# A third seven-product quad for the short convolution's x and C, earlier loads for the retention heads, and an earlier join in w_o

## The chip, the cores and the metric

The kernel runs on one core of one Trainium2 chip. The metric is the device time of one execution in microseconds. The median of three runs of the kernel before is 1023.01 us (1022.69 to 1025.45).

## The reference

One encoder block for x of 512 tokens by 1024 features, float32. Cut to what the change touches:

```python
h = rmsnorm(x, g_mix)
proj = h @ w_in
xc, gb, gc, q, k, v, g_sw, gate_a, gate_r = split(proj)
u = gc * xc
conv = sum over 3 taps of shifted u * w_conv[tap]
y_a = (gb * conv) @ w_a_out
ret = retention(rotary(q), rotary(k), v), 4 heads, normalised per head
y_r = (ret * g_ret * silu(g_sw)) @ w_r_out
x = x + (sigmoid(gate_a) * y_a + sigmoid(gate_r) * y_r) @ w_o
h2 = rmsnorm(x, g_ffn)
x = x + (silu(h2 @ w_ff_gate) * (h2 @ w_ff_up)) @ w_ff_down
y = rmsnorm(x, g_final)
```

xc, gb and gc are 1024 columns wide each; in the kernel they are x, B and C.

## The kernel before

**Numbers.** TensorE multiplies float32 in a rounded form (fp32r). To keep the accuracy, each operand is split into a high part (a cast, on ScalarE, L203) and a low part (the difference, on VectorE, L204), and each product is done by three matmuls: high by high, low by high, high by low (L342 to L344, or by helpers at L383 with 256 columns and L427 with 512). Weights come from memory into "raw" tiles (10 buffers, loads L286 and in `prefetch_block`) and are split into "whi" and "wlo" (a pool of 5 units). A unit can be written again when the last matmul that reads its old contents is done.

**Seven products.** Where two column groups of 256 features go with two halves of the tokens, four block products are replaced by Strassen's seven (a "quad"). Its weights are sums of quarters; `fm_quad` does it feature-major with 256 tokens wide matmuls, 24 for each of the seven products. The sums t1 to t4 are made either on VectorE while the weights lie in raw tiles (L301), or ahead of time in DRAM by accumulating DMAs of GpSimd (`sum_step`, L272 and L274) for the quads listed in `SUMMED`. The DMAs are issued a step at a time behind stores on GpSimd's queue.

**Stages.** (1) The projections of q, k, v, the swish gate and the branch gates go to DRAM tiles (qkd, vd, sgd, and gate tiles). (2) `mix_quads`: the short convolution is done in four parts of 256 features. For parts 1 and 2, a quad makes x and C of the part, VectorE multiplies them into u and convolves; then one quad makes B for both, which gives z; `z_forms` splits z into the forms that the product by w_a_out needs, and stores them in DRAM on GpSimd's queue (L633). (3) `load_head(0)` loads the first head's tables, q and k (high and low), v and gate on SyncE's queue; `do_scores` makes p = scores times decay, each of its four rows evicted by VectorE (L873) and split; `split_v` splits v. (4) `do_mix(2)`: part 3 of the convolution without a quad: x, C and B in one chunk each of 2 x 24 matmuls with 512 columns, from blocks of weights (wpack). (5) The head loop: `do_pv` multiplies p by v (48 matmuls; VectorE takes statistics and scales, L894 to L905), the next head's scores, and the product by w_r_out; part 4 of the convolution (`do_mix(3)`) lies in it. (6) w_a_out and the merge, seven products. (7) w_o, seven products, token-major: `join` (L1026) adds a product to the residual rows y of one tile of 128 tokens and one half of the features; `complete` stores the rows, squares them on ScalarE with the sum over the row (L1031), and when both halves are there adds the two sums and EPS (L1033 on GpSimd, L1035 on ScalarE), takes the power -1/2 on GpSimd (L1036) and scales the rows on VectorE (L1039); `tr_o` turns the scaled rows of one tile by eight 128 x 128 transposes of TensorE (L1053), and splits them into the feed-forward part's operands. (8) The feed-forward part, and the last norm.

**What sets the order.** The program is recorded in the order of the code and given to a scheduler, which puts each engine's instructions into one fixed queue; each engine works its queue in order, and waits by semaphores. `issue_after` ties an instruction's place behind another's. Large tiles come from a pool of 14 (`bigtile`), 512-column temporaries from one of 9 (`t512`), and there are 8 PSUM banks.

Of the kernel before, what the change touches and what calls it, by code (L numbers as in the profile page):

```python
# [12 lines left out]
F32 = mybir.dt.float32  # L13
# [56 lines left out]

def plan():
# [75 lines left out]
SUMMED = (("f", 0), ("f", 1), ("o",))  # L147
# [24 lines left out]
def block_kernel(ctx: ExitStack, tc: tile.TileContext, xw0, xw, xT, xtok, wpack, wquad, cols, decs, rot, g_ffn, g_final, out):  # L172
# [50 lines left out]

    made = []
# [7 lines left out]
    def prefetch_block(loads, splits):  # L232
# [29 lines left out]

    steps = {"quads": sums_of(SUMMED[:2]), "heads": sums_of(SUMMED[2:])}

# [15 lines left out]

    def load_raws(upto):
        while loaded[0] < len(LOADS) and LOADS[loaded[0]][0] <= upto:
# [462 lines left out]
    def do_quad(left, right, func, func_left=None):  # L745
        def ev_sum(dst, o, f):
            def ev(tt, t):
# [3 lines left out]
                if tt and not o:  # L751
                    sum_step(last)
# [36 lines left out]
    def z_forms(s, z):  # L789
# [3 lines left out]
        def put(j, t):  # L793
# [3 lines left out]
            for d, x in zip(zd[j], hl):  # L797
                store(d[:, :, s, :], x.bitcast(F32))
# [7 lines left out]
        put(3, x2[:, 1:2])  # L806

    def do_mix(s):
        us, c = [], bigtile()[:, 0:2, :]
        feature_major(xg, lambda m, ps: us.append(snap(ps)))  # L810
        u = u_tile()

        def ev_c(m, ps):
            nc.vector.tensor_tensor(out=u[:, m, 1:513], in0=ps, in1=us[m], op=ALU.mult)
            conv(m, 2 * s + m, u[:, m], c[:, m])
        feature_major(xg, ev_c)

        def ev_b(m, ps):
            nc.vector.tensor_tensor(out=c[:, m], in0=ps, in1=c[:, m], op=ALU.mult)
        feature_major(xg, ev_b)  # L820
        z_forms(s, c)
# [5 lines left out]

    def mix_quads():

        c = bigtile().rearrange("p (s m) t -> p s m t", s=2)  # L830
        for s in range(2):
            u, got = u_tile(), {}

            def ev21(ps):
                nc.vector.tensor_tensor(out=u[:, :, 257:513], in0=halves(ps), in1=halves(got["c2"]), op=ALU.mult)

            def ev12(t):
                nc.vector.tensor_tensor(out=u[:, :, 1:257], in0=halves(got["x1"]), in1=halves(t), op=ALU.mult)
            fm_quad(xf, lambda t: got.update(x1=t), ev21, lambda t: got.update(c2=t), ev12)
# [566 lines left out]
```

## Time and profile before

| | us |
|---|---|
| median of 3 runs | 1023.01 |
| profiled execution, its own time | 1025.12 |
| its span, first to last instruction | 1023.3 |
| TensorE busy (matmul) | 1014.1 |
| VectorE busy | 903.1 |
| ScalarE busy | 550.0 |
| GpSimd busy | 137.0 |

The mean granted clock of TensorE over the span is 0.997 of full speed. A row of a timeline has the start from the span's beginning, the duration, engine, line, operation, tiles (out<-in), the sizes and, in brackets, how long the engine was idle before it and what ended that. Durations of matmuls are those of one instruction on its way through the array; in a full queue the next starts sooner, so the distance of starts is the cost. In a row of windows stand the stretch, then busy time and count for PE, weight loads, DVE (VectorE), ACT (ScalarE) and POOL (GpSimd), then the granted clock, the share of the DMA engines and GB/s. A row of waits has the total, the count and the longest in us.

### The profile page before, as it was taken

Reading aid. Unit: us, or ns where it says so; the run is one execution under the profiler, and the core shown is the slowest. Engines: PE = TensorE matmul, PEld = TensorE weight load, DVE = VectorE, ACT = ScalarE, POOL = GpSimd, SP = SyncE. Lnnn points to the kernel's source line nnn. Section 1 sums busy time; section 2 is a strip of 40 time slices with the busy share of each in tenths; the row PEclk is TensorE's granted clock in tenths of the full one; section 3 lists DMA queues with packets and bytes.
Section 4 is the critical chain, followed back from the end, with each engine's and each line's share of the span. In section 5 each row is a group of like instructions: output and inputs, shape, how many; then the busy total and the mean of one; then the engine's idle time right before and its main releaser. Section 6 shows DMA issues by size and latency. Waiting matters only on the chain.

```text
span 1023.3 us, 14820 instructions
## 1 busy us (share of the span) xinstructions
PE 1014.1 (99%) x5586; PEld 884.6 (86%) x5586; DVE 903.1 (88%) x1161; ACT 550.0 (54%) x748; POOL 137.0 (13%) x225
## 2 busy tenths in 40 slices
PE   9999999999999999999999999999999999999997
PEld 7888888888888998888888888879998999899986
DVE  7877998979798988797989998999998999889996
ACT  7556655553656455343543335586654565556554
POOL 0020221222112003202122100020002000110011
PEclk9999999999999999999999999999999999999999
DMA  9525487694766657848597855473318522663533
GB/s 351 191 86 187 166 297 216 212 315 151 256 204 227 256 198 267 326 146 331 125 342 294 292 181 165 162 268 96 125 41 224 178 84 83 190 161 104 166 68 98
DMA packets 53352, 200.24 MB, mean 196 GB/s; under 512 B 7264, under 2 KB 7392, under 8 KB 48672
## 3 DMA queue, kind: packets, MB, share of 16 engines
q1 hardware_dynamic: 37600, 137.39, 38.8%
q0 software_dynamic: 15392, 61.62, 20.7%
q8 instruction: 44, 0.72, 0.3%
q10 hardware_dynamic: 288, 0.29, 0.1%
q14 instruction: 28, 0.23, 0.1%
HBM read 160.73 MB, written 55.31 MB: 211 GB/s over the span
## 4 chain that ended last, share of the span: by engine, by line
PE 93%; DVE 4%; issue 1%; ACT 1%; DMA 0%; POOL 0%; POOLq 0%; DVEq 0%; ACTq 0%
PE bank L427 35%; PE bank L383 28%; PE bank L342 10%; PE bank L344 10%; PE bank L343 10%; DVE wlo L204 1%; DVE xform L204 1%; DVE big L1026 1%; PE bank L477 0%; DMA ydr<-big 0%; DVE big L1006 0%; PE bank L662 0%; DVE big L980 0%; PE bank L1053 0%; DVE big L979 0%
## 5 line engine op out<-in xcount | busy, mean ns | idle before, releaser
L203 ACT CAST whi<-raw 128x1024 fp32r<-128x1024 f32 (+2 forms) x299 | 303.1, 1028 | 268.4 <-PE bank L427 64.7
L204 DVE TENSOR_TENSOR wlo<-raw,whi 128x1024 fp32r<-128x1024 f32 (+2 forms) x300 | 353.1, 1193 | 70.6 <-ACT whi L203 70.1
L383 PE MATMUL bank<-xform,whi 128*128 128x256 f32 x1424 | 258.8, 284 | 0.0
L383 PEld LDWEIGHTS bank<-xform,whi 128*128 128x128 f32 x1424 | 223.4, 193 | 0.9 <-ACT t L434 0.5
L383 PE MATMUL bank<-xform,wlo 128*128 128x256 f32 x712 | 201.6, 284 | 0.0
L427 PE MATMUL bank<-whi,big 128*128 128x512 f32 x596 | 187.6, 390 | 0.0
L427 PE MATMUL bank<-whi,xform 128*128 128x512 f32 x496 | 157.1, 390 | 0.0
L301 DVE TENSOR_TENSOR raw<-raw 128x1024 f32<-128x1024 f32 (+1 forms) x128 | 151.8, 1204 | 3.6 <-DMA raw<-wquad 2.7
L383 PEld LDWEIGHTS bank<-xform,wlo 128*128 128x128 f32 x712 | 137.1, 193 | 0.0
L427 PEld LDWEIGHTS bank<-whi,big 128*128 128x128 f32 x596 | 111.8, 188 | 24.2 <-ACT t L434 0.4
L427 PE MATMUL bank<-wlo,big 128*128 128x512 f32 x298 | 116.0, 389 | 0.0
L427 PEld LDWEIGHTS bank<-whi,xform 128*128 128x128 f32 x496 | 93.0, 188 | 19.6 <-DVE xform L204 0.4
L427 PE MATMUL bank<-wlo,xform 128*128 128x512 f32 x248 | 96.5, 389 | 0.0
L434 ACT COPY t<-bank 128x512 f32<-128x512 f32 x105 | 61.2, 586 | 56.0 <-PE bank L383 29.7
L342 PE MATMUL bank<-big,whi 128*128 128x512 f32 x220 | 85.7, 390 | 0.0
L344 PE MATMUL bank<-big,wlo 128*128 128x512 f32 x220 | 85.6, 389 | 0.0
L343 PE MATMUL bank<-big,whi 128*128 128x512 f32 x220 | 85.6, 389 | 0.0
L427 PEld LDWEIGHTS bank<-wlo,big 128*128 128x128 f32 x298 | 56.0, 188 | 11.4
L427 PEld LDWEIGHTS bank<-wlo,xform 128*128 128x128 f32 x248 | 46.6, 188 | 9.5
L342 PE MATMUL bank<-whi,big 128*128 128x512 f32 x128 | 49.8, 389 | 0.0
L343 PE MATMUL bank<-wlo,big 128*128 128x512 f32 x128 | 49.8, 389 | 0.0
L344 PE MATMUL bank<-whi,big 128*128 128x512 f32 x128 | 49.8, 389 | 0.0
(200 smaller groups left out, 1372.5 us busy)
## 6 DMA issues: line engine op xcount, KB each, us to landing
raw<-wquad SPq DMA_DIRECT2D x140, 512.0 KB, 4.6
raw<-wpack SPq DMA_DIRECT2D x42, 512.0 KB, 5.8
t_f<-wquad POOLq DMA_DIRECT2D x12, 512.0 KB, 6.9
z<-t POOLq DMA_DIRECT2D x24, 256.0 KB, 4.6
t_o<-wquad POOLq DMA_DIRECT2D x12, 512.0 KB, 6.9
zform<-z POOLq DMA_DIRECT2D x6, 1024.0 KB, 7.7
v<-t POOLq DMA_DIRECT2D x16, 256.0 KB, 5.2
sg<-t POOLq DMA_DIRECT2D x16, 256.0 KB, 4.8
```

The lines of the kernel that those rows point to most:

```text
L203: first = (round or nc.scalar.copy)(hi, src)
L204: low_of[0] = nc.vector.tensor_tensor(out=lo, in0=src, in1=hi.bitcast(F32), op=ALU.subtract)
L301: nc.vector.tensor_tensor(out=t, in0=t, in1=raws[quad, more, u][:, 0:n], op=ALU.add)
L342: nc.tensor.matmul(ps, lh, rh, start=first, stop=False)
L343: nc.tensor.matmul(ps, lh, rl, start=False, stop=False)
L344: nc.tensor.matmul(ps, ll, rh, start=False, stop=last)
L383: nc.tensor.matmul(o, l[:, c], r[:, k], start=start and s == 0 and k == 0 and i == 0, stop=stop and k == 3 and i == 2, skip_group_check=True)
L427: nc.tensor.matmul(pss[tt], l, r[:, c], start=start and k == 0 and i == 0, stop=stop and k == n - 1 and i == 2, skip_group_check=True)
L434: nc.scalar.copy(t, ps)
L1026: nc.vector.tensor_tensor(out=yt, in0=yt, in1=ps, op=op)
```

## The change

Four things are changed.

1. Part 3's x and C become a quad of their own (`XC`, `xc_quad(2)`), done by seven products between the second x-C quad and B's quad; its result waits in `part2`. `do_mix(2)` keeps only its B chunk. The sums of the new quad are made in DRAM by GpSimd, ahead of those of the feed-forward part, and a step follows each of the stores in the places named in the diff. In the list of weight blocks, part 3 keeps only B.
2. Head 0's q, k, v and gate are loaded on SyncE's queue among the raw loads of the later quads (every third), its table ahead of `z_forms`, and the blocks of weights are ordered behind them.
3. Head 1's q and k are loaded on GpSimd's queue behind the last store of `z_forms(1)`; the rest of that head's loads stay on SyncE's.
4. In w_o, `join` of the third tile stands ahead of `tr_o(1)`, and the add in `complete` goes from ScalarE to GpSimd.

```diff
+XC = ("x", C_XC + 512, C_GC + 512)
...
-    for c0, c1 in ((C_XC, C_GC), (C_XC + 256, C_GC + 256), (C_GB, C_GB + 256)):
+    for c0, c1 in ((C_XC, C_GC), (C_XC + 256, C_GC + 256), XC[1:], (C_GB, C_GB + 256)):
         for name in FORMS:
             out.append(("q", ("x", c0, c1), name, 0, 4))
     for s in (2, 3):
-        for c in (C_XC, C_GC, C_GB):
+        for c in (C_GB,) if s == 2 else (C_XC, C_GC, C_GB):
             a("w_in", c + s * 256)
...
-SUMMED = (("f", 0), ("f", 1), ("o",))
+SUMMED = (XC, ("f", 0), ("f", 1), ("o",))
...
-            nc.sync.dma_start(st[c], wpack[i][:, c * QH:(c + 1) * QH])
+            with tc.issue_after(behind[-1].ins) if behind else nullcontext():
+                nc.sync.dma_start(st[c], wpack[i][:, c * QH:(c + 1) * QH])
...
-    steps = {"quads": sums_of(SUMMED[:2]), "heads": sums_of(SUMMED[2:])}
+    steps = {"quads": sums_of(SUMMED[:1]) + sums_of(SUMMED[1:3]), "heads": sums_of(SUMMED[3:])}
...
-            nc.sync.dma_start(t[:, 0:n], src[:, 0:n])
+            raw = nc.sync.dma_start(t[:, 0:n], src[:, 0:n])
             raws[quad, name, u] = t
+            if among and loaded[0] % 3 == 0:
+                with tc.issue_after(raw.ins):
+                    among.pop(0)()
...
-                if tt and not o:
+                if tt:
                     sum_step(last)
...
+    def xc_quad(s, c):
+
+        u, got = u_tile(), {}
+
+        def ev21(ps):
+            nc.vector.tensor_tensor(out=u[:, :, 257:513], in0=halves(ps), in1=halves(got["c2"]), op=ALU.mult)
+
+        def ev12(t):
+            nc.vector.tensor_tensor(out=u[:, :, 1:257], in0=halves(got["x1"]), in1=halves(t), op=ALU.mult)
+        fm_quad(xf, lambda t: got.update(x1=t), ev21, lambda t: got.update(c2=t), ev12)
+        for m in range(2):
+            conv(m, 2 * s + m, u[:, m], c[:, m])
...
+        xc_quad(0, c[:, 0])
+        head = []
+        for src, dt in ((qkd[0][0], F32R), (qkd[0][1], F32R), (vd[0], F32), (sgd[0], F32)):
+            among.append(lambda src=src, dt=dt: head.append(load(src, dt)))
+        xc_quad(1, c[:, 1])
+        part2.append(bigtile()[:, 0:2, :])
+        xc_quad(2, part2[0])
...
         fm_quad(xf, times(0, T1), times(0, T2), times(1, T2), times(1, T1))
+        while among:
+            among.pop(0)()
+        tab = misctile(896, "tab")
+        nc.sync.dma_start(tab, tabs[0])
         for s in range(2):
-            z_forms(s, c[:, s])
...
+            stored = z_forms(s, c[:, s])
+        with tc.issue_after(stored.ins):
+            second.extend(load(t, F32R, nc.gpsimd) for t in qkd[1])
+
+        behind.append(last[3])
+        return head[0:2], tab, *head[2:]
+
+    def do_mix(s):
+        if s == 2:
+            c = part2[0]
+        else:
...
-    mix_quads()
-    nxt = load_head(0)
+    nxt = mix_quads()
     p = do_scores(nxt[0], nxt[1])
...
-            nxt = load_head(h + 1)
+            nxt = load_head(h + 1, second if h == 0 else None)
...
-        nc.scalar.activation(ac[:, 4:5], ac[:, 1:2], AF.Identity, bias=ac[:, 3:4])
+        nc.gpsimd.tensor_tensor(out=ac[:, 4:5], in0=ac[:, 1:2], in1=ac[:, 3:4], op=ALU.add)
...
     def ev(tt):
+        join(2 + tt, 0, a[tt])
         if tt == 0:
             tr_o(1)
-        join(2 + tt, 0, a[tt])
         complete(2 + tt, 0, 1)
     prod_tm(4, of(M["a22"]), a, False, True, ev)
```

Where instructions stand now, first on ScalarE between the last forms of z's second part and the product of head 0. The casts from `t512` tiles to big_3566 (big_3816 in the changed program) make the high part of p, those to big_3612 (big_3862) the high part of v, and those to whi weights. Before:

```order
L203 CAST t512_3550<-big_2814 128x256
L203 CAST big_3566<-t512_3575 128x512
L203 CAST big_3566<-t512_3586 128x512
L203 CAST big_3612<-big_3562 128x1024
L203 CAST big_3566<-t512_3597 128x512
L203 CAST big_3612<-big_3562 128x1024
L203 CAST big_3566<-t512_3608 128x512
L434 COPY t512_3656<-bank_3631 128x512
L203 CAST whi_3696<-raw_3689 128x1024
```

And now:

```order
L207 CAST t512_3806<-big_2826 128x256
L207 CAST whi_4144<-raw_4137 128x1024
L207 CAST whi_4209<-raw_4205 128x1024
L207 CAST big_3816<-t512_3825 128x512
L207 CAST big_3816<-t512_3836 128x512
L207 CAST big_3816<-t512_3847 128x512
L207 CAST big_3816<-t512_3858 128x512
L207 CAST big_3862<-big_3337 128x1024 x2
L207 CAST t512_3934<-big_3296 128x512
```

Two casts of weights, for the chunks of part 4, have moved ahead of p's and v's casts. whi_4209 is written into the unit that held whi_3695, the last weights of part 3's B chunk.

VectorE at the same place, from the first eviction of the scores on. Before:

```order
L873 SCALAR_TENSOR_TENSOR t512_3575<-bank_3568,tab_3556 128x512
L873 SCALAR_TENSOR_TENSOR t512_3586<-bank_3579,tab_3556 128x512
L873 SCALAR_TENSOR_TENSOR t512_3597<-bank_3590,tab_3556 128x512
L204 TENSOR_TENSOR big_3567<-t512_3575,big_3566 128x512
L204 TENSOR_TENSOR big_3567<-t512_3586,big_3566 128x512
L873 SCALAR_TENSOR_TENSOR t512_3608<-bank_3601,tab_3556 128x512
L204 TENSOR_TENSOR big_3567<-t512_3597,big_3566 128x512
L204 TENSOR_TENSOR big_3613<-big_3562,big_3612 128x1024
```

And now, from the last eviction on, with bank_3880 and bank_3906 the two banks of the B chunk:

```order
L912 SCALAR_TENSOR_TENSOR t512_3858<-bank_3851,tab_3750 128x512
L885 TENSOR_TENSOR big_3296<-bank_3880,big_3296 128x512
L797 MEMSET u_4202 128x2
L798 MEMSET u_4202 128x2
L208 TENSOR_TENSOR wlo_4145<-raw_4137,whi_4144 128x1024
L885 TENSOR_TENSOR big_3296<-bank_3906,big_3296 128x512
L208 TENSOR_TENSOR wlo_4210<-raw_4205,whi_4209 128x1024
L208 TENSOR_TENSOR big_3817<-t512_3825,big_3816 128x512
L208 TENSOR_TENSOR big_3817<-t512_3836,big_3816 128x512
L208 TENSOR_TENSOR big_3817<-t512_3847,big_3816 128x512
L208 TENSOR_TENSOR big_3817<-t512_3858,big_3816 128x512
L208 TENSOR_TENSOR big_3863<-big_3337,big_3862 128x1024 x2
```

The low parts of p and v, which alternated with the evictions of the scores, now stand behind both evictions of the B chunk and two weight splits.

The last place is VectorE at tr_o(1) in w_o, where L1026 (L1064) is `join` and L1039 (L1077) the scaling. Before:

```order
L1039 SCALAR_TENSOR_TENSOR t_5916<-big,ac,gb 128x512
L1026 TENSOR_TENSOR big<-big,bank 128x512
L204 TENSOR_TENSOR xform<-bank,xform 128x4x128 x2
L204 TENSOR_TENSOR wlo<-raw,whi 128x1024
L204 TENSOR_TENSOR xform<-bank,xform 128x4x128 x2
L1026 TENSOR_TENSOR big<-big,bank 128x512 x2
L204 TENSOR_TENSOR wlo<-raw,whi 128x1024 x2
L1039 SCALAR_TENSOR_TENSOR t_6030<-big,ac,gb 128x512
```

And now:

```order
L208 TENSOR_TENSOR xform<-bank,xform 128x4x128 x2
L208 TENSOR_TENSOR wlo<-raw,whi 128x1024
L1064 TENSOR_TENSOR big<-big,bank 128x512
L208 TENSOR_TENSOR xform<-bank,xform 128x4x128 x2
L1064 TENSOR_TENSOR big<-big,bank 128x512
L208 TENSOR_TENSOR wlo<-raw,whi 128x1024
L1077 SCALAR_TENSOR_TENSOR t_6136<-big,ac,gb 128x512
```

The third tile's join stands ahead of the two splits of tr_o(1), and one weight split fewer stands between the joins and the scaling.

More of the change, by code (lines that the diff above doesn't have):

```diff
@@ L1 @@
-from contextlib import ExitStack
+from contextlib import ExitStack, nullcontext
 import numpy as np
@@ L222, in block_kernel @@
     block = [0]
+    behind = []
     made = []
@@ L279, in block_kernel @@
     loaded = [0]
+    among = []
     def load_raws(upto):
@@ L805, in z_forms @@
         put(2, w)
[L806 to L821, printed above, removed]
+        return put(3, x2[:, 1:2])
     T1, T2 = slice(0, 256), slice(256, 512)
@@ L826, in halves @@
         return t.rearrange("p (m t) -> p m t", m=2)
+    def xc_quad(s, c):
[7 more added lines that the diff above has]
+            conv(m, 2 * s + m, u[:, m], c[:, m])
+    part2, second = [], []
     def mix_quads():
         c = bigtile().rearrange("p (s m) t -> p s m t", s=2)
[L831 to L839, printed above, removed]
-            for m in range(2):
-                conv(m, 2 * s + m, u[:, m], c[:, s, m])
+        xc_quad(0, c[:, 0])
[5 more added lines that the diff above has]
+        xc_quad(2, part2[0])
         def times(s, t):
```

23 lines of the change are left out of this document (18 added, 5 removed).

## The prediction, as put on record before the changed kernel ran

> **What bounds the kernel now.** The page comes first: engines, then the chain that ended last.
>
> ```profile
> span 1023.3 us, 14820 instructions
> ...
> PE 1014.1 (99%) x5586; PEld 884.6 (86%) x5586; DVE 903.1 (88%) x1161; ACT 550.0 (54%) x748; POOL 137.0 (13%) x225
> ...
> PE 93%; DVE 4%; issue 1%; ACT 1%; DMA 0%; POOL 0%; POOLq 0%; DVEq 0%; ACTq 0%
> ```
>
> TensorE is busy 99% of the span and makes up 93% of the chain. So an edit pays only if it takes matmuls away or takes away a wait of TensorE, and it costs only if it makes such a wait. The price of a matmul is read from long pieces of the chain in which nothing else stands:
>
> ```profile
> 73.07 152.35 PE bank L427 x672
> ...
> 323.39 55.13 PE bank L383 x456
> ```
>
> 152.35/672 = 0.2267 us for a 512-column matmul and 55.13/456 = 0.1209 us for a 256-column one. Next, all waits of TensorE that the trace holds, and the one in mid-kernel in TensorE's timeline with the windows around it:
>
> ```profile
> PE bank L1053 <- DVE t L1039: 1.6, 1, 1.6
> PE bank L477 <- DVE t L474: 1.4, 1, 1.4
> ```
>
> ```profile
> 686.51 0.28 PE L383 MATMUL bank<-xform,wlo 128*128 128x256 f32 x1
> 688.40 1.71 PE L1053 MATMUL bank<-ident,t 128*128 128x128 f32 x8 [1.61 <-DVE t L1039]
> 689.76 0.77 PE L383 MATMUL bank<-xform,whi 128*128 128x256 f32 x2
> ...
> 692.82 0.27 PE L383 MATMUL bank<-xform,wlo 128*128 128x256 f32 x1
> ```
>
> ```profile
> 680.00:700.00 20.00, 18.30 (x129) 17.30 (x128) 17.55 (x23) 15.12 (x29) 1.79 (x3) 0.91 0.51 171
> 700.00:720.00 20.00, 20.00 (x167) 19.89 (x166) 19.75 (x20) 13.60 (x16) 0.00 (x0) 1.00 0.47 146
> ```
>
> The second wait is the kernel's start, which the change leaves alone. The first is tr_o(1) waiting for the scaled rows of the third tile. TensorE could have gone on at 686.51 + 0.12 = 686.63 and went on at 688.40: 1.77 us idle. Behind it the matmuls are about twice as far apart until 692.82, and the mean granted clock of these 20 us is 0.91, where the next row has 1.00. 9% of 20 us is 1.8 us lost to a clock at half speed, near the half of the 3.4 us from 689.4 to 692.8 (1.7). That stall cost 1.8 + 1.7 = 3.5 us in this execution.
>
> **The change part by part.** The sum is made against the profiled execution's own time, 1025.12 us.
>
> *Matmuls.* The x and C chunks of part 3 go: 2 x 48 x 0.2267 = 21.8 us. Seven products of 24 come: 168 x 0.1209 = 20.3 us. **-1.5 us.**
>
> *The stall at tr_o(1).* Before, what the third tile's scaling waits for reads so, on VectorE, ScalarE and GpSimd:
>
> ```profile
> 680.06 1.28 DVE L204 TENSOR_TENSOR xform<-bank,xform 128x512 fp32r<-128x512 f32 x2
> 681.26 1.21 DVE L204 TENSOR_TENSOR wlo<-raw,whi 128x1024 fp32r<-128x1024 f32 x1
> ...
> 683.59 1.27 DVE L1026 TENSOR_TENSOR big<-big,bank 128x512 f32<-128x512 f32 x2
> ...
> 687.59 1.41 DVE L1039 SCALAR_TENSOR_TENSOR t<-big,ac,gb 128x512 f32<-128x512 f32 x2 [0.46 <-POOL ac L1036]
> ```
>
> ```profile
> 683.66 1.10 ACT L1059 COPY big<-bank 128x512 f32<-128x512 f32 x2
> 684.61 0.68 ACT L1031 ACTIVATE t<-big 128x512 f32<-128x512 f32 x1
> ...
> 685.24 1.08 ACT L203 CAST whi<-raw 128x1024 fp32r<-128x1024 f32 x1
> 686.17 0.33 ACT L1035 ACTIVATE ac<-ac 128x1 f32<-128x1 f32 x1
> ```
>
> ```profile
> L1033 POOL TENSOR_SCALAR ac<-ac 128x1 f32<-128x1 f32 x4 | 1.7, 415 | 75.1 <-ACT t L1031 75.1
> ...
> L1036 POOL TENSOR_TENSOR ac<-ac,mhalf 128x1 f32<-128x1 f32 x4 | 3.6, 900 | 14.3 <-ACT ac L1035 14.3
> ```
>
> The square was done by about 685.2; the add (L1035) stood behind a weight cast of ScalarE and ended at 686.5; the power on GpSimd came then. In the new order the third tile's join follows the weight split, so it ends near 682.4 + 0.6 = 683.0 instead of 684.2; ScalarE has one copy ahead of the square instead of two, so the square ends near 684.1 + 0.7 = 684.8. The add is then GpSimd's own: no row shows this add there, the nearest is L1033's 0.42 us, so I take 0.4 (0.2 to 1.0, the end from the power's 0.9). The power takes 0.9: 686.1. VectorE has by then the splits, the other join and a weight split behind it (683.0 + 1.2 + 0.6 + 1.2 = 686.0), and the first scaled half took 688.40 - 687.59 = 0.8 us to reach TensorE: 687.0, against 686.63. So 0.4 us of idle stay (0 to 1.0), and I take the clock as kept, since nothing in the trace shows a lowered clock behind so short a gap: 3.5 - 0.4 = **-3.1 us.**
>
> *A new stall at head 0's pv.* This is where most of the gain goes. Between the scores of head 0 and its pv stood three chunks, 144 x 0.2267 = 32.6 us, in which ScalarE and VectorE made the high and low parts of p and v:
>
> ```profile
> 389.80 0.39 PE L342 MATMUL bank<-big,whi 128*128 128x512 f32 x1
> ...
> 400.23 0.39 PE L343 MATMUL bank<-big,whi 128*128 128x512 f32 x1
> ...
> 422.44 0.39 PE L342 MATMUL bank<-big 128*128 128x512 f32 x1
> ```
>
> ```profile
> 397.26 1.22 ACT L203 CAST big<-t 128x512 fp32r<-128x512 f32 x2 [1.40 <-DVE t L873]
> 398.38 1.05 ACT L203 CAST big<-big 128x1024 fp32r<-128x1024 f32 x1
> 399.33 0.61 ACT L203 CAST big<-t 128x512 fp32r<-128x512 f32 x1
> ...
> 401.80 1.05 ACT L203 CAST whi<-raw 128x1024 fp32r<-128x1024 f32 x1
> ```
>
> ```profile
> 398.33 1.28 DVE L204 TENSOR_TENSOR big<-t,big 128x512 fp32r<-128x512 f32 x2
> ...
> 402.47 1.22 DVE L204 TENSOR_TENSOR big<-big 128x1024 fp32r<-128x1024 f32 x1
> ```
>
> VectorE was through at 403.7, 19 us ahead of the pv at 422.44: that was the cover. Now one chunk is left, 48 x 0.2267 = 10.9 us, so in this trace's clock TensorE has its last matmul of the chunk at 389.80 + 47 x 0.2267 = 400.45 and wants pv's first product at 400.68. What decides is ScalarE's order. Before, p's casts stand ahead of the weight casts; in the changed program two weight casts stand ahead of p's. The second goes to the buffer that the chunk's own last weights lie in, so it waits for the last matmul but one (400.23 + 0.39 = 400.6). Before, ScalarE stood the same way in front of weight casts at this stage, with nothing urgent behind them:
>
> ```profile
>   PE bank L343: 10.9, 4
> ```
>
> That is 10.9 us of idle in four waits between 395 and 425 us, all for TensorE's middle product. Behind the waiting cast stand now four casts of p and two of v: 400.65 + 0.95 + 4 x 0.56 + 1.05 = 404.9 is when the first matmul of pv may start (0.56 is half the step from 397.26 to 398.38, 0.95 the step from 398.38 to 399.33). **4.2 us of idle.** Then four matmuls run (0.9 us, to 405.8), and the fifth needs the low part of v. VectorE has its own weight split ahead (behind the same cast: 401.7 + 1.15), four low parts of p at 0.6 and one of v at 1.2: 406.5. **0.7 us more.** It is 4.9 us in all, 4.2 if VectorE's part is hidden, 5.3 with all casts and splits at their full durations. On top comes the clock: 1.77 us of idle cost 1.7 us of it in this execution, so I take 1.7 for this longer stall, and 1.0 to 2.6 as bounds, by where the 3.4 us of half speed fall: into the idle itself, or twice. **+6.6 us** (5.2 to 7.9).
>
> The Trainium skill ("TensorE: Matmul & The Clock Gate", section "The HAM clock gate") has the clock fall after a whole idle window of about 3.4 us, with windows that run freely. The row above has it fall after 1.77 us, so I go by the row. By the page's rule, as an estimate from its 3.4 us, 4.2 us of idle hold a whole window only in (4.2 - 3.4)/3.4, about one case in four, and the sum would mostly be 1.7 us lower.
>
> *What is hidden.* The rows are GpSimd's issues of the sums of before, what transfers between 280 and 440 us took to land, and two windows there (the share of the DMA engines is last but one):
>
> ```profile
> L272 POOL DMA_DIRECT2D t_f<-wquad x8 | 7.0, 874 | 0.2
> ```
>
> ```profile
> raw<-wquad SPq DMA_DIRECT2D x11, 512.0 KB, 4.5
> ...
> big<-ql SPq DMA_DIRECT2D x2, 1024.0 KB, 10.5
> ```
>
> ```profile
> 360.00:380.00 20.00, 20.00 (x162) 19.49 (x160) 17.46 (x22) 10.76 (x14) 0.00 (x0) 1.00 0.47 161
> 380.00:400.00 20.00, 20.00 (x111) 17.49 (x111) 17.51 (x31) 8.79 (x16) 10.55 (x16) 1.00 0.94 334
> ```
>
> GpSimd's last stores of z in that stage:
>
> ```profile
> 395.95 2.55 POOL L633 DMA_DIRECT2D z<-t  x4 [0.37 <-ACT t L203]
> ```
>
> The new quad's sums are 8 steps more on GpSimd at 0.9 us each, far ahead of their use. Its seven weight splits replace four, 3 x 1.2 us more on VectorE (3 x 1.05 on ScalarE); VectorE idles 2.5 us of 20 here, and the new quad lacks the adds (L301) that the two others make on VectorE, so this is covered; if it weren't, TensorE would wait for about one split. Head 0's loads go among the raw loads and the weight loads behind them, in a stretch where the DMA engines are half busy. Head 1's q and k go behind the last store of z on GpSimd's queue (395.95 + 2.55 = 398.5) and land near 398.5 + 10.5 = 409; head 1's scores follow pv, whose 48 matmuls (10.9 us) end after 416. All this I cost at nothing; a raw load that came late would cost up to its landing, 4.5 us.
>
> **Sum.** -1.5 - 3.1 + 6.6 = +2.0 us: 1027.1 on the profiled execution's time. That time is 2.1 us above the median shown, 1023.01, and two of the three runs shown lie 2.1 to 2.4 below it. If that distance has nothing to do with the stall, the median becomes 1025.0. If those runs did not lose the clock at tr_o(1) (1.7 us, most of the distance), only 1.4 of the 3.1 was there to save, and it becomes 1026.7. The rows can't tell; between the two I forecast **1025.7**, no difference that can be measured or just about one (0.3%, 3.1 us, is what a measurement tells from no change).
>
> **Rivals.** (1) *The saving at tr_o(1) comes back in the feed-forward part's forms: slower.* TensorE comes 3 us earlier to the first pair's products, whose forms VectorE makes; the windows row from 700 to 720 has VectorE busy for 19.75 of 20 us, and the row before has only 2.45 us in which it idles. For it: there is next to no slack. Against it: VectorE waited too in the old stall and starts earlier by 1 to 1.5 us as well. It decides as soon as a form's low part ends later than TensorE comes; its price is up to the 3 us saved: 1027 to 1028.8. (2) *The stall at pv isn't there*, since p is ready by another way than the order says: then -1.5 - 3.1 and, by the same halving, about 1019.3. For it: p's own inputs are ready near 399.6, ahead of 400.68. Against it: the casts stand in one queue behind the waiting one. (3) *The clock stays up through pv's stall*, because it falls in two windows: 1025.7 - 1.7 = 1024.0; the trace has one case of idle in mid-kernel, and it speaks against it. The rule of the Trainium skill above ("TensorE: Matmul & The Clock Gate") would mostly give this case. (4) *Quad 2 is late*, because its sums or raw loads are: one landing of 7 us and a lost clock, 1031 or more. No wait of TensorE in the present quads speaks for it.
>
> **How the numbers follow.** Forecast 0.52 (1024 to 1027.2), (1) 0.20, (2) 0.13, (3) 0.10, (4) 0.05. Slower by over 0.3% is above 1026.1: (1), (4) and two fifths of the forecast, 0.46. Faster is below 1019.9: most of (2), 0.10. The rest, 0.44, is within. The range leaves out (4), the far end of (1) and half of (2): 1019.5 to 1028.7.
>
> **What would show it.** TensorE's waits name v's cast (ScalarE) and v's low part (VectorE) at head 0's pv with 4 to 5 us together, and the granted clock there falls below 1; at tr_o the wait is under 1 us and the clock 1.00. If the wait at pv is absent, the reading of ScalarE's queue was wrong; if one appears at the first pair, rival 1 holds; any wait in the third quad is rival 4.

## The result, and the profile after

The changed kernel took 1028.66 us (median of 6 runs, 1027.38 to 1031.26) where the kernel before took 1023.06 (6 runs beside it). The ratio is 1.0055 with an interval of [1.0043, 1.0066]: slower by about half a per cent. The profiled execution of it took 1031.26 us by its own time, 6.14 more than the profiled one of before. In e8 below, one execution of six, 2609.34 us, was in a slow state and is left out of its numbers. The page, in its first lines and the chain's shares by engine:

```profile
span 1029.5 us, 14980 instructions
...
PE 1015.1 (99%) x5658; PEld 887.4 (86%) x5658; DVE 907.8 (88%) x1167; ACT 552.2 (54%) x748; POOL 146.6 (14%) x239
...
PE 96%; DVE 2%; DMA 1%; issue 1%; ACT 0%; POOL 0%; POOLq 0%; DVEq 0%; ACTq 0%
```

TensorE still makes up nearly the whole chain, so the loss must be in its waits and in its clock. All its waits in the changed kernel:

```profile
PE bank L354 <- ACT big L207: 3.9, 1, 3.9
PE bank L395 <- ACT whi L207: 1.7, 1, 1.7
PE bank L489 <- DVE t L486: 1.4, 1, 1.4
PE bank L1091 <- DVE t L1077: 0.5, 1, 0.5
```

The third is the start, as before. The fourth is the turning of the third tile, 1.6 before and 0.5 now. (These transposes are `tr_o(2)` in the code: they stand behind the first 24 matmuls of the feed-forward part, and wait for the scaled rows of the third tile. The texts above and some expectations below call the place tr_o(1), which is the call that the third tile's join was moved ahead of.) The first is head 0's pv, as forecast. The second wasn't forecast. The feed-forward part goes in three groups of gate and up products with 256 columns (L383, now L395), each followed by 512-column products (L427, now L439), which are `down` for the first two; the wait lies near the start of the second group and is for a weight cast. Where in the span the time comes is read by setting the same places of both programs side by side. In TensorE's timeline of before these are the first transposes in w_a_out, the last turning of w_o, the first product of the first `down`, the first of the second `down`, and the last matmul:

```profile
629.17 1.03 PE L998 MATMUL bank<-ident,big 128*128 128x128 f32 x8
...
694.01 1.03 PE L1053 MATMUL bank<-ident,t 128*128 128x128 f32 x8
...
758.51 0.40 PE L427 MATMUL bank<-whi,big 128*128 128x512 f32 x1
...
862.79 0.40 PE L427 MATMUL bank<-whi,big 128*128 128x512 f32 x1
...
1016.84 0.39 PE L427 MATMUL bank<-whi,big 128*128 128x512 f32 x1
```

And in that of the changed kernel, with tr_o(2) as the second row:

```profile
633.72 1.03 PE L1036 MATMUL bank<-ident,big 128*128 128x128 f32 x8
...
691.88 1.38 PE L1091 MATMUL bank<-ident,t 128*128 128x128 f32 x8 [0.53 <-DVE t L1077]
...
695.98 1.04 PE L1091 MATMUL bank<-ident,t 128*128 128x128 f32 x8
...
761.12 0.40 PE L439 MATMUL bank<-whi,big 128*128 128x512 f32 x1
...
868.67 0.40 PE L439 MATMUL bank<-whi,big 128*128 128x512 f32 x1
...
1022.62 0.39 PE L439 MATMUL bank<-whi,big 128*128 128x512 f32 x1
```

The differences, after less before, are +4.55, +3.48 (691.88 against 688.40), +1.97, +2.61, +5.88 and +5.78. So w_a_out's transposes are reached 4.55 us late. About 6.1 of it are lost at pv (below), and the rest is a gain of 1.57: pv was wanted at 420.87, against 422.44 before. That isn't all due to the matmuls. A piece of 672 matmuls that the change doesn't touch, at 73.07 before, already starts 0.46 us earlier here:

```profile
72.61 152.49 PE bank L439 x672
```

Over the profiles its place varies by about 1.2 us (72.27 in e12, 73.46 in e6), in no order that follows the changes. So 1.1 us are left for the seven products. At tr_o(2) 1.07 comes back as a shorter wait, and 1.51 behind it, since the clock stays up. The rest of the first group gives 0.64 of it away, the second group costs 3.27, and little changes from there to the last matmul. Behind it the span is 0.4 longer (6.46 us before, 6.88 after). It is 6.5 in e1 and e2 too, and 6.8 to 6.9 in all the others, which have the new quad; nothing here explains that.

TensorE at pv in the changed kernel, the last matmul of B's chunk first:

```profile
420.64 0.39 PE L356 MATMUL bank<-big,wlo 128*128 128x512 f32 x1
424.96 1.63 PE L354 MATMUL bank<-big 128*128 128x512 f32 x4 [3.93 <-ACT big L207]
426.74 0.80 PE L355 MATMUL bank<-big 128*128 128x512 f32 x1
...
428.99 0.39 PE L354 MATMUL bank<-big 128*128 128x512 f32 x1
```

It wanted pv's first product at 420.87 and had it at 424.96, 4.1 us idle; the fifth came 0.9 us after the fourth would have let it; from 426.74 to 428.99 five matmuls took 2.25 us in place of 1.13, at half the clock. That is 6.1 in all. The 0.9 us go with the end of VectorE's low part of v at 426.7, but the list of waits doesn't show them as a wait, since the four matmuls ahead were drawn out too (1.63 us); e3 and e4 show 0.2 and 0.6 there. ScalarE and VectorE at that place:

```profile
418.12 1.05 ACT L207 CAST whi<-raw 128x1024 fp32r<-128x1024 f32 x1 [2.90 <-PE bank L355]
420.84 1.04 ACT L207 CAST whi<-raw 128x1024 fp32r<-128x1024 f32 x1 [1.67 <-PE bank L355]
421.79 2.17 ACT L207 CAST big<-t 128x512 fp32r<-128x512 f32 x4
423.87 1.99 ACT L207 CAST big<-big 128x1024 fp32r<-128x1024 f32 x2
```

```profile
421.92 1.23 DVE L208 TENSOR_TENSOR wlo<-raw,whi 128x1024 fp32r<-128x1024 f32 x1 [0.16 <-ACT whi L207]
423.06 2.49 DVE L208 TENSOR_TENSOR big<-t,big 128x512 fp32r<-128x512 f32 x4
425.47 2.35 DVE L208 TENSOR_TENSOR big<-big 128x1024 fp32r<-128x1024 f32 x2
```

Both weight casts wait for TensorE's matmuls, the second till the chunk's end, and p's and v's casts stand behind them. VectorE does the same with the low parts. The windows around pv, tr_o(2) and the second group's wait:

```profile
420.00:440.00 20.00, 15.92 (x63) 12.27 (x62) 17.08 (x33) 9.26 (x14) 7.28 (x12) 0.91 0.94 354
...
680.00:700.00 20.00, 19.37 (x137) 17.69 (x136) 19.17 (x27) 16.31 (x30) 3.76 (x7) 1.00 0.67 220
780.00:800.00 20.00, 18.25 (x97) 15.76 (x96) 15.84 (x17) 7.66 (x11) 5.26 (x6) 0.91 1.05 246
```

The granted clock is 0.91 at pv and in the second group and 1.00 at tr_o(2), where it was 0.91 before.

The unforeseen stall is read from the chain of waits, back from TensorE's late matmul at 793.46:

```profile
777.13 1.30 DVE t L460 x2
778.43 1.14 DVE wlo L208
...
779.60 6.88 DMA raw<-wquad
...
789.91 2.37 DVE raw L313 x2
...
792.36 1.05 ACT whi L207
```

Two evictions stand ahead of a weight split; the split frees a raw buffer; the load into that buffer is issued then, takes 6.88 us, and the sums and the cast made from it are late. VectorE in the kernel before, at the same place:

```profile
772.91 2.96 DVE L204 TENSOR_TENSOR wlo<-raw,whi 128x1024 fp32r<-128x1024 f32 x3 [1.34 <-ACT whi L203]
775.79 1.28 DVE L448 TENSOR_TENSOR t<-bank,t 128x512 f32<-128x512 f32 x2
```

There three splits come ahead of the evictions, in the changed kernel two. The diff has no line in the feed-forward part; the scheduler moved the split. How long TensorE then waits goes with the load: in e10 (the changed kernel again) and e1 the order is the same, the load takes 5.35 and 5.20 us, and the wait is 0.3 and 0.2.

### The profile page after: what moved, and what is told of

Same layout as the page of the kernel before. It is cut to its first block, busy times and chain, and to the rows that moved or that the text cites. A ratio compares the mean times of both kernels' runs of the same rounds, so it can differ in the third digit from the quotient of the medians.

```text
span 1029.5 us, 14980 instructions
## 1 busy us (share of the span) xinstructions
PE 1015.1 (99%) x5658; PEld 887.4 (86%) x5658; DVE 907.8 (88%) x1167; ACT 552.2 (54%) x748; POOL 146.6 (14%) x239
## 4 chain that ended last, share of the span: by engine, by line
PE 96%; DVE 2%; DMA 1%; issue 1%; ACT 0%; POOL 0%; POOLq 0%; DVEq 0%; ACTq 0%
PE bank L439 38%; PE bank L395 29%; PE bank L355 9%; PE bank L356 9%; PE bank L354 9%; DMA raw<-wquad 1%; PE bank L489 0%; PE bank L1091 0%; DVE raw L313 0%; DVE big L208 0%; PE bank L1036 0%; DVE wlo L208 0%; ACT whi L207 0%; PE bank L674 0%; DVE big L1316 0%
## 5 line engine op out<-in xcount | busy, mean ns | idle before, releaser
L207 ACT CAST whi<-raw 128x1024 fp32r<-128x1024 f32 (+2 forms) x302 | 306.4, 1028 | 272.5 <-PE bank L439 67.3
L395 PE MATMUL bank<-xform,whi 128*128 128x256 f32 x1488 | 271.3, 285 | 1.8 <-ACT whi L207 1.7
L395 PEld LDWEIGHTS bank<-xform,whi 128*128 128x128 f32 x1488 | 233.4, 193 | 3.5 <-ACT whi L207 2.1
L395 PE MATMUL bank<-xform,wlo 128*128 128x256 f32 x744 | 210.5, 284 | 0.0
L439 PE MATMUL bank<-whi,big 128*128 128x512 f32 x596 | 186.9, 389 | 0.0
L439 PE MATMUL bank<-whi,xform 128*128 128x512 f32 x496 | 157.1, 390 | 0.0
L395 PEld LDWEIGHTS bank<-xform,wlo 128*128 128x128 f32 x744 | 143.3, 193 | 0.0
L439 PEld LDWEIGHTS bank<-whi,big 128*128 128x128 f32 x596 | 111.9, 188 | 23.8 <-ACT t L446 0.4
L439 PE MATMUL bank<-wlo,big 128*128 128x512 f32 x298 | 115.7, 389 | 0.0
L439 PEld LDWEIGHTS bank<-whi,xform 128*128 128x128 f32 x496 | 93.0, 188 | 19.7 <-DVE xform L208 0.6
L439 PE MATMUL bank<-wlo,xform 128*128 128x512 f32 x248 | 96.5, 389 | 0.0
L354 PE MATMUL bank<-big,whi 128*128 128x512 f32 x188 | 73.3, 390 | 0.0
L356 PE MATMUL bank<-big,wlo 128*128 128x512 f32 x188 | 73.2, 389 | 0.0
L355 PE MATMUL bank<-big,whi 128*128 128x512 f32 x188 | 73.1, 389 | 0.0
L439 PEld LDWEIGHTS bank<-wlo,big 128*128 128x128 f32 x298 | 56.0, 188 | 11.4
L439 PEld LDWEIGHTS bank<-wlo,xform 128*128 128x128 f32 x248 | 46.6, 188 | 9.6
## 6 DMA issues: line engine op xcount, KB each, us to landing
zform<-z POOLq DMA_DIRECT2D x6, 1024.0 KB, 7.0
```

Source lines behind the costliest of these rows:

```text
L207: first = (round or nc.scalar.copy)(hi, src)
L354: nc.tensor.matmul(ps, lh, rh, start=first, stop=False)
L355: nc.tensor.matmul(ps, lh, rl, start=False, stop=False)
L356: nc.tensor.matmul(ps, ll, rh, start=False, stop=last)
L395: nc.tensor.matmul(o, l[:, c], r[:, k], start=start and s == 0 and k == 0 and i == 0, stop=stop and k == 3 and i == 2, skip_group_check=True)
L439: nc.tensor.matmul(pss[tt], l, r[:, c], start=start and k == 0 and i == 0, stop=stop and k == n - 1 and i == 2, skip_group_check=True)
```

## The experiments

**e1: part 4 of the change alone,** on the kernel before:

```diff
-        nc.scalar.activation(ac[:, 4:5], ac[:, 1:2], AF.Identity, bias=ac[:, 3:4])
+        nc.gpsimd.tensor_tensor(out=ac[:, 4:5], in0=ac[:, 1:2], in1=ac[:, 3:4], op=ALU.add)
...
+        join(2 + tt, 0, a[tt])
         if tt == 0:
             tr_o(1)
-        join(2 + tt, 0, a[tt])
```

> The kernel before with the fourth part of the change alone (third tile's join ahead of tr_o(1), the add on GpSimd). Theory A: the wait of TensorE in the feed-forward part (1.7 us, products behind the first down) comes from this part: it makes the scheduler put one weight split behind two evictions there. Then the wait at tr_o falls from 1.6 to at most 0.6 us, a wait of about 1.7 us for a weight cast appears near 787 us, and the two cancel: within 2 us of before. Theory B: that wait is chance or comes from the new quad's traffic: no such wait here, 1.4 to 3.1 us faster than before.

It took 1025.69 (12 runs), ratio 1.0014 [1.0002, 1.0025]. Six of the runs lie between 1023.0 and 1025.0, six between 1026.4 and 1027.8. The profiled one (1023.36) has 0.5 us at tr_o(2) and 0.2 in the second group, where theory A wanted 1.7. Its order on VectorE has the displaced split, and so has the built order of each half of part 4 alone; without part 4 (e3) it is gone. So part 4 moves it: theory A is right on the order, and the wait of 1.7 us isn't in this profile. The mean granted clock is 0.997 in each of the upper six and 0.998 to 0.999 in the lower, so the upper six lost clock somewhere. That they lost it at this stall is likely, but not shown: the one profile taken is of the lower six.

**e2: e1 with that split back ahead of the evictions:**

```diff
+        if late:
+            prefetch()
...
-            nc.vector.tensor_tensor(out=p1[tt], in0=b[tt], in1=p1[tt], op=ALU.add)
+            with tc.issue_after(lows[-1]) if late else nullcontext():
+                nc.vector.tensor_tensor(out=p1[tt], in0=b[tt], in1=p1[tt], op=ALU.add)
```

> The same, with that one weight split put ahead of the two evictions again (a prefetch call moved, nothing else). Theory A: the wait in the feed-forward part is gone and the gain at tr_o stays: 1.3 to 3.1 us faster than before. Theory B: the same time as the run with the fourth part alone, within 1 us.

1022.51 (11 runs, 1021.95 to 1023.27), ratio 0.9989 [0.9981, 0.9998]. The upper group is gone, and the only waits left are 1.4 and 0.5. The medians of e1 and e2 are 3.2 us apart, but e1's lies between its two groups: the lower six (median 1023.4) are 0.9 above e2, the upper six (1026.7) 4.2. The wait is gone as by theory A; the gain of 1.0 us on the medians is below the 1.3 to 3.1 expected. Part 4 by itself is worth about 1 us, not 3.

**e3: the changed kernel without part 4** (e1's diff taken back).

> The changed kernel without its fourth part: quad, early loads and head 1's loads alone. Theory A: waits of 3.9 us at head 0's pv and 1.6 us at tr_o, none in the feed-forward part: before -1.4 +6.1 = 4.7 us slower than before (3.5 to 6). Theory B: the wait in the feed-forward part is there too: 6 to 8.5 us slower.

1028.81 (6 runs), ratio 1.0058 [1.0041, 1.0076]; 3.9 and 0.2 at pv, 1.6 at tr_o(2), none in the second group. That is theory A, 5.3 us slower on the medians. Two readings of it matter. The window of tr_o(2):

```profile
680.00:700.00 20.00, 18.30 (x128) 16.61 (x127) 18.66 (x25) 16.40 (x32) 3.84 (x5) 1.00 0.65 219
```

The same 1.6 us of waiting as before, with the clock at 1.00: a stall of this length costs the clock in some executions and not in others. And the stretch from the last turning to the first `down`:

```profile
697.04 1.04 PE L1091 MATMUL bank<-ident,t 128*128 128x128 f32 x8
...
761.53 0.40 PE L439 MATMUL bank<-whi,big 128*128 128x512 f32 x1
```

It lasts 64.49 us here, 64.50 before and 65.14 in the changed kernel, e1 and e2, which have part 4. So the 0.64 given back in the first group goes with part 4. It is lost in gaps of 0.2 us or less between matmuls, which the list of waits leaves out; what they wait for is not shown.

**e4: the changed kernel with e2's order,** and **e10: the changed kernel once more.**

> The changed kernel with that one weight split put ahead of the two evictions. Theory A: no wait in the feed-forward part, 1.7 to 3.5 us faster than the changed kernel (1025 to 1027). Theory B: the same as the changed kernel, within 1 us.

> The changed kernel once more, beside e8 and e9 on the same chip, for more of its times. If the late weight split in the feed-forward part costs 3.5 us in each run, its median lies about 3 us above that of e4 (1028.8); if most runs lose a part of that at pv in any case and the rest is spread, the two medians lie within 1 us of each other, and times between 1027 and 1031.5 appear in both.

e4: 1028.8 (6 runs, 1027.4 to 1030.4), ratio 1.0045 [1.0031, 1.0058]; no wait in the second group. e10: 1028.38 (5 runs, 1027.75 to 1030.04), ratio 1.0037 [1.0024, 1.005]; its profiled execution (1028.12) waits there for 0.3 us only. (The runs of before beside e8, e9 and e10 have a median of 1025.62, seven of eleven of them above 1025, where those beside e4 have 1023.51; so the ratios of these three are low against the others.) So the 1.7 us with its lost clock in the first profile of the changed kernel is a rare case there: of its 11 runs, two (1031.17 and 1031.26) are that long. Mending the order doesn't move the median measurably: theory A of e4 fell, theory B holds, and e10's second case with it. Part of the spread of the rest is the clock at pv; e4's profile has this window:

```profile
420.00:440.00 20.00, 15.52 (x55) 11.79 (x54) 16.85 (x34) 9.26 (x14) 7.51 (x13) 0.83 0.95 365
```

Lost at pv, against a spacing of 0.2267 us, are 6.1, 6.2, 7.9 and 5.8 us in the profiles of the changed kernel, e3, e4 and e10. A clock of 0.83 is 3.4 us lost in 20, 0.91 is 1.8; the difference, 1.6, is nearly what e4 loses more than the others.

**e5: e4 with head 1's q and k back on SyncE's queue; e6: head 0's loads back too.**

```diff
-        with tc.issue_after(stored.ins):
-            second.extend(load(t, F32R, nc.gpsimd) for t in qkd[1])
...
-            nxt = load_head(h + 1, second if h == 0 else None)
+            nxt = load_head(h + 1)
```

> The kernel of e4 with the third part of the change undone: head 1's q and k are loaded on SyncE's queue with the rest of that head, and two large buffers aren't taken before p's and v's. In its order p's and v's casts stand ahead of the waiting weight cast again, and the low parts of p and v ahead of the B chunk's evictions. Theory C: it is this part, not the shorter cover by itself, that makes the stall at head 0's pv. Then 1.0 to 1.7 us of it are left (the first low part of v, at 402.0 in the time of before, against TensorE at 400.9), with the clock kept: 1021.5 to 1023, some 6 us faster than e4. Theory D: the quad alone makes it, since 22 us of cover are gone: 1026 or more, wait at pv over 3 us.

> The kernel of e4 with the second and third parts undone: all of head 0's loads behind z_forms again and head 1's on SyncE's queue; the quad, the join, the add and the mended feed-forward order stay. Theory C: as e5 within 1 us, since the early loads hide nothing that was bare. Rival: head 0's q and k now come late for its scores, with a wait of TensorE for a load there: slower than e5 by that wait, 2 us or more.

e5: 1031.38, ratio 1.0071 [1.0059, 1.0083]. e6: 1030.44, ratio 1.0064 [1.0051, 1.0078]. The stall at pv got longer, 4.0 and 1.8 us of waiting in e5, 4.2 and 2.7 in e6. So theory D holds and theory C fell, though in e5 p's casts stand ahead of the weight casts again, and the low parts of p and v ahead of the chunk's evictions. e6 is 0.9 below e5, as its own theory C had it: the early loads of head 0 (part 2) gain nothing that these runs show. In e5 VectorE stood behind z's stores, which hold the temporaries that z's next forms and the scores are written to:

```profile
419.78 0.69 DVE L209 TENSOR_TENSOR t<-t,t 128x512 fp32r<-128x512 f32 x1 [5.19 <-DMA z<-t]
```

The transfers issued between 400 and 420 us, with the median time to landing last, in e5:

```profile
z<-t POOLq DMA_DIRECT2D x11, 256.0 KB, 8.6
...
big<-qh SPq DMA_DIRECT2D x1, 1024.0 KB, 8.7
```

And in the changed kernel:

```profile
z<-t POOLq DMA_DIRECT2D x12, 256.0 KB, 4.3
...
big<-qh POOLq DMA_DIRECT2D x1, 1024.0 KB, 7.5
```

The stores land in 4.3 to 5.2 us in the three profiles whose loads start behind them (the changed kernel, e4 with 4.9, e10) and in 8.6 and 9.0 in e5 and e6, whose loads start beside them. So part 3 is worth about 2.6 us at this place (1031.38 against 1028.8), and the loads are not what makes the stall.

**e8: the two weight splits behind v's parts.** e4 with the splits of part 4's B weights tied behind v's last cast and low part, and the next scores behind pv's matmuls:

```diff
+        hold[:] = [cast.ins, low_of[0].ins]
...
-            split(st[c], hi, lo)
+            with ExitStack() as after:
+                n_held[0] += bool(hold)
+                for ins in hold if 3 < n_held[0] < 6 else ():
+                    after.enter_context(tc.issue_after(ins))
+                split(st[c], hi, lo)
...
-            p = do_scores(nxt[0], nxt[1])
+            with tc.issue_after(lastmm[0].ins) if h == 0 else nullcontext():
+                p = do_scores(nxt[0], nxt[1])
```

> The kernel of e4 with only the order at head 0's pv changed: the two splits of B's weights that stand ahead of p's casts on ScalarE and among p's low parts on VectorE are issued behind v's casts and low part. Theory A (the 4.1 us at pv are the two weight casts, which ScalarE takes in order ahead of p's): the wait for ScalarE falls from 3.9 to under 1 us, since p's last score was scaled at 420.0 us and four casts of 0.54 and one of 1.0 end at 421.6; the first wait for VectorE then stays at about 0.9 and the time falls by some 3 us to 1025.5. Theory B (the stall is VectorE's chain, and the casts only stand at its front): VectorE still has to evict the last chunk (421.7 to 422.4), make p's four low parts (2.5 us) and v's (1.2 us), which ends at about 426, so the wait for VectorE grows to about 3.4 us, and the two waits together fall only from 5.0 to about 4.0; the time falls by 1 us or less, to about 1028. A new wait of up to 1 us at B's second matmul group, whose low weights come later, is possible under both.

1030.69 (median of 5 runs, 1028.86 to 1033.77), ratio 1.0059 [1.0041, 1.0076], no better than e4. TensorE, and VectorE beside it:

```profile
421.16 1.19 PE L363 MATMUL bank<-big 128*128 128x512 f32 x4
425.55 0.80 PE L364 MATMUL bank<-big 128*128 128x512 f32 x1 [3.19 <-DVE big L209]
```

```profile
421.26 0.69 DVE L897 TENSOR_TENSOR big<-bank,big 128x512 f32<-128x512 f32 x1 [1.14 <-PE bank L365]
421.87 2.48 DVE L209 TENSOR_TENSOR big<-t,big 128x512 fp32r<-128x512 f32 x4
424.28 2.35 DVE L209 TENSOR_TENSOR big<-big 128x1024 fp32r<-128x1024 f32 x2
```

The wait for ScalarE is gone: pv starts with 0.1 us of delay. But VectorE evicts the chunk's second bank only when its last matmul is done, and p's four low parts and v's stand behind that, so v's low part is ready at 425.5 and TensorE waits 3.2 us there; 5.2 are lost at pv. The weight splits that were held back make a new wait of 1.8 us at the next chunk. Theory B holds for the waits, though its time (about 1028) was missed by more than 2 us: the casts only stood at the front of a stall that VectorE's chain has by itself.

**e7: the scores written ahead of z's forms.**

```diff
-        for s in range(2):
-            stored = z_forms(s, c[:, s])
-        with tc.issue_after(stored.ins):
-            second.extend(load(t, F32R, nc.gpsimd) for t in qkd[1])
+        second.extend(load(t, F32R, nc.gpsimd) for t in qkd[1])
...
-        return head[0:2], tab, *head[2:]
+        p = do_scores(head[0:2], tab)
+        vv = split_v(head[2])
+        for s in range(2):
+            z_forms(s, c[:, s])
+        return p, vv, head[3]
```

> The kernel of e4 with head 0's scores and v's split written ahead of z_forms, and head 1's q and k on GpSimd's queue ahead of the stores of z. p's and v's parts are then ready before the B chunk ends (near 395 in the time of before, by 4 evictions and 4 low parts of 0.6 us and two of 1.2). If the stall at pv is a matter of what stands ahead of these parts, it is gone altogether: before -1.4 (matmuls) -1.1 (join) = 1021, no wait of TensorE over 0.6 us in mid-kernel. If the stall needs the shorter cover only, there is still one of over 2 us. Side effect to watch: the stores of z later, and with them w_a_out's loads, not before 500 us.

1024.1 (11 runs), ratio 1.0002 [0.9994, 1.0011]. Nothing is lost at pv, as expected of what stands ahead of p's and v's parts; the time, 1021 by the expectation, was missed by 3 us. A new wait stands at the first output product, because VectorE waits for z's stores in part 4's forms, ahead of head 1's normalization and transposes. VectorE and TensorE:

```profile
481.45 0.42 DVE L209 TENSOR_TENSOR t<-big,t 128x256 fp32r<-128x256 f32 x1 [3.98 <-DMA z<-t]
...
495.06 11.44 DVE L223 STREAM_TRANSPOSE big<-big 32x512 f32<-32x512 f32 x16
```

```profile
509.62 0.50 PE L356 MATMUL bank<-big 128*128 128x512 f32 x1 [1.74 <-ACT big L979]
```

**e9: e7 with the forms of parts 3 and 4 behind the next head's scores.**

> The kernel of e7 with the later forms of z (of parts 2 and 3 of the mixing) written behind the next head's scores too, as those of part 1 and 2 of the first group already are. Theory A (e7's new wait of 1.7 us at 509.6 us comes from VectorE standing 4 us behind z's stores at 481 us): the wait is gone, no new one of over 0.5 us takes its place, and the time is that of e7 less 1.7 to 3.5 us, 1020.8 to 1022.5, since the 1.4 us of matmuls and the 1.1 us at tr_o are then no longer given back. Theory B (VectorE and ScalarE simply have no room for head 1's work there): a wait of 1 to 3 us stays near the same place, perhaps for another tile, and the time stays at 1023.5 to 1024.5.

1029.38 (6 runs), ratio 1.0044 [1.0031, 1.0057]. Both theories missed. The forms now stand between the scores and the transposes, 14 of the 16 of which run from 499.8 us on, and the wait at the first output product grows to 4.3 us.

**e11 and e12: only part 4's forms moved, behind the transposes** (e11 behind the first output product, e12 ahead of it):

```diff
-        z_forms(s, c)
+        if s == 2:
+            z_forms(s, c)
+        else:
+            late.append(c)
...
             do_wr(h - 1, yr)
+            if late:
+                z_forms(3, late.pop())
```

> The kernel of e7 with the fourth part's z forms written behind the first output product of head 0 (behind head 1's transposes on VectorE, where e7 has them ahead of head 1's normalization). Theory A (VectorE's 4.0 us behind z's stores at 481 us are what makes e7's transposes and with them ysum's copies late): the transposes start at least 5 us earlier, the 1.7 us at the first output product are gone, the waits left are those at the start and at tr_o (1.4 and 0.5), and the time is that of e7 less 1.7 to 3.5 us: 1020.6 to 1022.4, below e2. Theory B: the same stores now hold VectorE up by 2 to 4 us ahead of the weight splits of head 1's part of the next products, and a wait of 1 to 3 us stands there; the time stays at 1023 to 1025.

> As e11, but the fourth part's z forms written directly behind head 1's transposes, ahead of the output product. By theory A of e11 it does the same, with the scaling of the transposed tile 1 to 2 us later: 1020.6 to 1023. By theory B the wait is longer than in e11, since two of the weight splits stand behind the stores: 2 to 5 us, 1024 to 1028.

e11: 1021.77 (8 runs, 1021.49 to 1022.33), ratio 0.9972 [0.9962, 0.9983]. e12: 1021.96 (11 runs), ratio 0.9981 [0.9972, 0.999]. In e11 the transposes start some 5 us sooner, and TensorE's waits are the start and tr_o(2) only:

```profile
490.45 10.00 DVE L223 STREAM_TRANSPOSE big<-big 32x512 f32<-32x512 f32 x14
```

```profile
PE bank L494 <- DVE t L491: 1.4, 1, 1.4
PE bank L1099 <- DVE t L1085: 0.5, 1, 0.5
```

Theory A holds for both. e11 beats the kernel before by 1.9 us on the medians and the changed one by about 6.7. Its last matmul (1013.30) is 1.7 us ahead of e2's (1015.01); 0.6 of that stands already at the piece of 672 matmuls (72.78 against 73.39), so 1.1 are the seven products'. On the medians e11 is 0.7 ahead of e2, and the span behind the last matmul takes 0.4 of the 1.1.

## Why the prediction came out as it did

*The number.* 1028.66 lies inside the stated 1019.5 to 1028.7 by 0.04 us. It lies outside the 1024 to 1027.2 that the forecast itself was given, in the band that rival 1 was priced at (1027 to 1028.8), though what came back in rival 1's place is 0.64 us and not up to 3. So the mechanism at pv was forecast, and that the number fell into the range is in part luck.

*Matmuls, -1.5.* Right in sign, a little large: 1.1 in the first pair of profiles, and 1.1 in e11 against e2, where nothing takes it back.

*pv, +6.6 (5.2 to 7.9).* Right in place, order and size: 4.1 us of idle for ScalarE where 4.2 was forecast, 0.9 ahead of the low part of v where 0.7 was, and the clock below 1; 5.8 to 7.9 in four profiles. But the prediction's cause was only half of it. It put 4.2 us on two weight casts in front of p's and 0.7 on VectorE. e8 takes the casts away and 3.2 us move to VectorE, where p's and v's low parts come behind the chunk's last eviction. That order isn't the whole either: e5 has the low parts ahead of the evictions, and there VectorE waits for z's stores first. Common to all of them is that, with one chunk of cover, the work on p and v comes behind z's forms and isn't done in time; e7, e11 and e12 end the stall by making the scores ahead of z's forms.

*tr_o(2) (called tr_o(1)), -3.1.* The wait was sized right (0.5 left, forecast 0.4). The clock was mis-sized: 1.7 us of half speed belong to the profiled execution, not to the median one. Of 69 further runs of the kernel before, 46 lie at 1022.4 to 1024.0, with a mean granted clock of 0.998 or 0.999, and 23 at 1025.0 to 1026.2, all with 0.997. The profiled execution, 1025.12 with 0.997, is of the minority, and e3 shows the same wait without the loss. So against the median there were 1.1 us to save, and 0.64 came back in the first group. That has rival 1's place and a fifth of its price; that it is VectorE's forms that come late there, as rival 1 says, isn't shown. The prediction saw both ends, 1025.0 and 1026.7, and went between them; 1026.7 was the one to take.

*What was costed at nothing.* The feed-forward part's order failed here. The prediction followed part 4 through w_o and didn't look at what the scheduler did 90 us later. One split moved behind two evictions: 3.27 us in the profiled execution, 0.3 in e10's. On the rest the cover held: no wait in the third quad (rival 4), and head 1's loads behind the stores show no cost; they save 2.6 us against loads beside them.

*The sum against the median.* 1023.0 - 1.1 - 1.1 + 0.64 + 6.0 + 0.3 + 0.4 = 1028.1, e10's profiled 1028.12. Against the forecast that is 2.4 more: 1.0 for going between the two ends, 0.3 since tr_o(2) had 1.1 to save and not 1.4, 0.4 for the matmuls, 0.6 in the first group, 0.3 in the second and 0.4 behind the last matmul, less 0.6 at pv. What is left to the median, about half a microsecond, lies within the spread of pv's clock, which took up to 1.8 us more (e4); no run here isolates it.

*The clock.* Waits of TensorE of 3.2 to 4.3 us lost the clock in all eight profiles that have one: the window is 0.91 at pv in the changed kernel, e3, e8 and e10, 0.83 in e4 and e5, 0.74 in e6 (e5 and e6 have a second wait right behind), and 0.83 at the output product in e9. Waits of 1.6 to 1.8 us lost it in two of five: tr_o(2) before and the second group after, but not tr_o(2) in e3, the output product in e7 or the next chunk in e8, all three with 1.00 in their window. The Trainium skill ("TensorE: Matmul & The Clock Gate", section "The HAM clock gate") has it fall after a whole idle window of about 3.4 us, with windows that run freely. The runs fit windows that a program meets differently from execution to execution, and not the length: 1.77 us of idle were enough in the profile of before. Rival 3, which followed from that rule, fell.

## What to carry to other kernels

A saved stall is to be priced from the median execution: where the profiled one is longer than the median, look first whether its clock loss is part of the difference. When a change takes away work that covered something, list every engine's queue between the last input and the first use; taking away the one that shows as the releaser may only hand the wait to the next. And when a scheduler orders the program, compare the built orders to the end, behind the lines that the diff touches too.

## What the runs showed of the hardware

Two 1 MB loads started beside a row of 256 KB stores, on another queue, went with a time to landing of 8.6 us for the stores (e5), against 4.9 in the same kernel with the loads started behind them (e4). The executions of the kernel before fall into two groups some 2.4 us apart (46 and 23 of 69), and the mean granted clock tells them apart without exception, 0.998 or 0.999 against 0.997. The same 1.6 us of waiting was followed by a lost clock in one profile (before) and not in another (e3). And a stretch that no change touches starts at 72.3 to 73.5 us of the span, so differences of a microsecond between two profiles are to be read from a place behind the start.
